# A transformer block on one core: first modulation chunk ahead of the inputs, squares summed on VectorE, one chunk ahead in a forced order, twelve ring slots

## The chip, the cores and the metric

One core of a Trainium2 chip runs the kernel. The metric is the device time of one execution in microseconds (us); lower is better. The kernel before takes 1745.03 us (median of 3 runs, 1744.43 to 1747.97).

## The reference, cut to what matters

The reference is one block of a diffusion transformer (256 tokens of x, 256 of a context, width 2048): a recurrent branch, windowed attention, a gated merge and a convolutional feed-forward, all in fp32. Only its beginning concerns this change:

```
mod = silu(cond) @ w_ada + b_ada              # six vectors of 2048, for x and for the context
def rms_norm(x, gain):   x * rsqrt(mean(x * x) + EPS) * gain
def modulate(x, gain, shift, scale):   rms_norm(x, gain) * (1 + scale) + shift
pc = modulate(ctx, norm1_g, mod_c[0], mod_c[1]) @ w_in
px = modulate(x,   norm1_g, mod_x[0], mod_x[1]) @ w_in
```

## The kernel before

Activations lie transposed: width on the 128 partitions (16 tiles, `kt`), 512 tokens (x, then context) in the free dimension. A fp32 product is taken as three products of fp32r parts: each operand is split into a high part (a cast on ScalarE) and a low part (a subtraction on VectorE); `mm3` (line 71) issues high by high, high by low, low by high. A tile framework plans the order of each engine's queue by priority, which is the order of the program text; `tc.high_priority(offset=n)` moves what stands in it n places ahead, and `tc.issue_after(ins)` queues what stands in it behind `ins` on its engine. Each engine then works through its queue in order, and SyncE's queue of transfers too.

*The modulation.* Shift and scale (4096 columns of `w_ada`) are made in eight chunks. Chunk j gives the columns of the two width tiles 2j and 2j+1, takes eight transfers of 512 KB (`ada_load`, line 170) and 32 TensorE instructions in four column groups (`ada_mm`, line 173). `mod_chunk` (line 178) copies the four rows of partial sums to SBUF, turns them into columns by products with `sel`, which also adds the four groups, and forms `acol` and `bcol` (scale with gain, and shift). Then it multiplies each x tile by the row `rs` of reciprocal norms, applies `acol` and `bcol` on ScalarE (two halves: x and context) and splits the result into `xhi` and `xlo`.

*The norm.* `x_part` (line 199) loads four x tiles by one transfer of 1 MB; ScalarE squares each tile, and a TensorE product with a matrix of ones adds it over partitions and tiles into `ssq`; `rsqrt` (line 139) makes `rs` by Ln and Exp.

*Order at the start.* Eight ring slots (two tiles of four) hold one chunk. Chunk 0's transfers are mixed with the inputs'; chunk 1 follows and is modulated (lines 206 to 220) before the j loop.

*The first products.* The loop at line 267 runs j = 0 to 7 over pairs of width tiles. `unit_v` (24 products into four PSUM banks that stay open over all j) and `unit_f` (18 products into three banks) use tiles 2j and 2j+1. Their weights come through `st.load` (line 105): a transfer, a cast and a subtraction. In between stand the two halves of chunk j+2's products and, at the end of the round, its `mod_chunk`: the modulation runs two chunks ahead. The order of the weight file `wst` (line 922) is the order of the loads.

After the loop TensorE goes on with 16-tile sums (`tform`, line 345) for the rest of the block; the other four modulation vectors are summed on VectorE meanwhile from the transfers `araw` (line 294).

Of the kernel before, what the change touches and what calls it, by code (L numbers as in the profile page):

```python
# [27 lines left out]
RUSH = 120  # L28
# [23 lines left out]
def block_kernel(ctx, tc, xct, prm, cst, ada2, wst, out):  # L52
    nc = tc.nc
    V, S, PE = nc.vector, nc.scalar, nc.tensor

    cons = ctx.enter_context(tc.tile_pool(name="cons", bufs=1))
    big = ctx.enter_context(tc.tile_pool(name="big", bufs=1))
    strm = ctx.enter_context(tc.tile_pool(name="strm", bufs=3))
    scr = ctx.enter_context(tc.tile_pool(name="scr", bufs=3))
    tiny = ctx.enter_context(tc.tile_pool(name="tiny", bufs=8))  # L60
    mm = ctx.enter_context(tc.tile_pool(name="mm", bufs=5, space=bass.MemoryType.PSUM))
    ms = ctx.enter_context(tc.tile_pool(name="ms", bufs=3, space=bass.MemoryType.PSUM))

    def bank(pool=None):
        pool = pool or mm
        return pool.tile([P, 512], F32, name="bank" + ("m" if pool is mm else "s"))

    def mmul(o, l, r, start, stop):
        PE.matmul(o, l, r, start=start, stop=stop, skip_group_check=True)  # L69

    def mm3(o, lh, ll, rh, rl, start, stop):
        mmul(o, lh, rh, start, False)
        mmul(o, lh, rl, False, False)
        mmul(o, ll, rh, False, stop)

    def smalltile(w, name="tn"):
        return tiny.tile([P, 32], F32, name=name)[:, 0:w]
# [79 lines left out]
    slots = [r[:, i, :] for r in ring for i in range(4)]  # L157


    csr = big.tile([P, KT, 32], F32, name="csr", tag="acc")  # L160
# [3 lines left out]
    sel = smalltile(2, "sel")  # L164
    V.tensor_tensor(sel, ident[:, 0:2], ident[:, 32:34], op=ALU.add)
    V.tensor_tensor(sel, sel, ident[:, 64:66], op=ALU.add)
    V.tensor_tensor(sel, sel, ident[:, 96:98], op=ALU.add)
    rs = scr.tile([P, 512], F32, name="rs", bufs=1)

    def ada_load(i):  # L170
        st.load_raw(slots[i])

    def ada_mm(aps, half):
        for kt in range(8 * half, 8 * half + 8):
            g = 32 * (kt % 4)
            mmul(aps[g:g + 32, :], csr[:, kt, :], slots[kt // 2][:, kt % 2 * 512:kt % 2 * 512 + 512], kt < 4, kt >= KT - 4)

    def mod_chunk(j, aps):
        rows = scr.tile([P, 512], F32, name="t")
        S.copy(rows, aps)  # L180
        for q in range(4):
            mmul(aps[:, 2 * q:2 * q + 2], rows[:, q * P:q * P + P], sel, q == 0, True)
        a4 = aps[:, 0:8].rearrange("p (q c) -> p q c", c=2)
        js = slice(2 * j, 2 * j + 2)
        V.tensor_tensor(bcol[:, js, :], a4[:, 0:2, :], bsh[:, js, None].broadcast_to([P, 2, 2]), op=ALU.add)
        V.tensor_tensor(acol[:, js, :], a4[:, 2:4, :], bsc[:, js, None].broadcast_to([P, 2, 2]), op=ALU.add)
        V.tensor_tensor(acol[:, js, :], acol[:, js, :], par("n1g")[:, js, None].broadcast_to([P, 2, 2]), op=ALU.mult)
        for kt in range(2 * j, 2 * j + 2):
            hn = scr.tile([P, 512], F32, name="t")
            V.tensor_tensor(hn, xraw[:, kt, :], rs, op=ALU.mult)  # L190
            for cnd in range(2):
                sl = slice(T * cnd, T * cnd + T)
                S.activation(hn[:, sl], hn[:, sl], AF.Identity, bias=bcol[:, kt, cnd:cnd + 1],
                             scale=acol[:, kt, cnd:cnd + 1])
            split(xhi[:, kt, :], xlo[:, kt, :], hn)

    ssq = bank()

    def x_part(i):
        nc.sync.dma_start(xraw[:, 4 * i:4 * i + 4, :], xct[:, 4 * i:4 * i + 4, :])  # L200
        for kt in range(4 * i, 4 * i + 4):
            sq = scr.tile([P, 512], F32, name="t")
            S.activation(sq, xraw[:, kt, :], AF.Square)
            mmul(ssq, ones, sq, kt == 0, kt == KT - 1)

    for i in range(8):
        ada_load(i)
        if i % 2:
            x_part(i // 2)
    for j in range(2):  # L210
        if j:
            for i in range(8):
                ada_load(i)
        aps = bank(ms)
        for half in range(2):
            ada_mm(aps, half)
        with tc.high_priority(offset=0 if j else RUSH):
            if not j:
                rsqrt(rs, ssq, 1.0 / D)
            mod_chunk(j, aps)  # L220
    base[0] = tc.tile_snap_priority()
    early_v = [bank() for _ in range(4)]

# [19 lines left out]
    def unit_v(j):  # L243
        st.load()
        return [st.next(4) for _ in range(2)]

    def unit_v_mm(j, wv, tts):
        for tt in tts:
            ts = slice(tt * P, tt * P + P)
            for k2 in range(2):  # L250
                kt = 2 * j + k2
                mm3(early_v[tt], xhi[:, kt, ts], xlo[:, kt, ts], *wv[k2], kt == 0, kt == KT - 1)
# [12 lines left out]


    for j in range(8):
        more = j < 6
        aps = bank(ms) if more else None
        wv = unit_v(j)  # L270
        if more:
            for i in range(4):
                ada_load(i)
        unit_v_mm(j, wv, range(4))
        if more:
            ada_mm(aps, 0)
        w = unit_f(j)
        if more:
            for i in range(4, 8):
                ada_load(i)  # L280
        unit_f_mm(j, w)
        if more:
            ada_mm(aps, 1)
            mod_chunk(j + 2, aps)
# [241 lines left out]
    kT = big.tile([P, 2, 512], F32, name="kT", tag="kT")  # L526
    va = big.tile([P, 4, 256], F32, name="va", tag="va")
# [50 lines left out]
    for h in range(H):  # L578
# [147 lines left out]
    ssa = scr.tile([P, 512], F32, name="rs", bufs=1)  # L726
# [22 lines left out]
    for j in range(W0, KT):  # L749
        o = tform(yb)  # L750
# [220 lines left out]
```

## Time and profile before

| | before |
|---|---|
| median of 3 runs | 1745.03 us |
| profiled execution | 1748.49 us |
| its span, first to last instruction | 1746.6 us |
| mean granted TensorE clock (share of 2.4 GHz) | 0.996 |
| TensorE matmul busy | 1719.9 us (98%) |
| VectorE busy | 1197.0 us (69%) |
| ScalarE busy | 847.6 us (49%) |
| mean DMA rate over the span | 213 GB/s |

PE is TensorE's matmul side, PEld its weight loads, DVE VectorE, ACT ScalarE, SP SyncE. All helpers record line 69 for a matmul, so groups of products are told apart by their tiles: `ringv,csr` and `ringq,csr` are the modulation, `t,cst` the norm, `sel,t` the turning of its rows, `whi,hl` and `wlo,hl` unit_v, `hl,whi` and `hl,wlo` unit_f and later sums. fp32 operands that are not fp32r take two instructions for one product.

### The profile page before, as it was taken

To read this page: it belongs to the slowest core of one execution; us is meant where nothing else is said; L and a number is where in the kernel's file an instruction comes from. 1 tells how busy PE (TensorE), PEld (TensorE's weight loads), DVE (VectorE), ACT (ScalarE), POOL (GpSimd) and SP (SyncE) were. 2 spreads that over 40 slices of the span, in tenths; PEclk is the share of its full clock that TensorE was granted. 3 is DMA by queue.
4 is the path that set the end of the run, shared out by engine and by line. 5 is a ranking of instruction groups with operands and counts; after the bars stand their busy time and mean duration, and the time that the engine had idled before them with its cause. 6 is when DMAs were issued, how large, how long until landed. Compare 5 with 4: busy or idle time off the path is not lost.

```text
span 1746.6 us, 24907 instructions
## 1 busy us (share of the span) xinstructions
PE 1719.9 (98%) x9562; PEld 1451.9 (83%) x9562; DVE 1197.0 (69%) x1807; ACT 847.6 (49%) x1292; POOL 68.4 (4%) x132
## 2 busy tenths in 40 slices
PE   7999999999999999999999999999999999999999
PEld 2567888888888888888888898888888888888887
DVE  1335967464669878697878797788766656666665
ACT  4335554252545755454455475555555334554332
POOL 0000100000000001010100000000000000000000
PEclk9999999999999999999999999999999999999999
DMA  9795744433436558686876567677755555555554
GB/s 374 297 364 184 265 143 157 161 117 117 136 104 214 202 189 289 233 309 237 304 249 231 190 215 256 228 239 262 233 183 186 188 185 188 183 192 182 190 196 145
DMA packets 103432, 371.85 MB, mean 213 GB/s; under 512 B 11280, under 2 KB 13712, under 8 KB 102800
## 3 DMA queue, kind: packets, MB, share of 16 engines
q1 hardware_dynamic: 84880, 303.14, 49.2%
q0 software_dynamic: 18432, 67.12, 11.8%
q8 instruction: 75, 1.23, 0.3%
q14 instruction: 45, 0.37, 0.1%
HBM read 368.11 MB, written 2.10 MB: 212 GB/s over the span
## 4 chain that ended last, share of the span: by engine, by line
PE 93%; DMA 4%; DVE 1%; issue 1%; ACT 0%; SPq 0%; DVEq 0%; POOLq 0%
PE bankm L69 84%; PE banks L69 6%; DMA araw<-in_ada_dram 3%; DVE wlo L111 1%; PE banks L493 0%; DMA raw<-in_wst_dram 0%; DVE acc L309 0%; DMA xraw<-in_xct_dram 0%; PE banks L666 0%; PE banks L317 0%; PE banks L485 0%; PE banks L475 0%; PE banks L522 0%; ACT whi L110 0%; PE banks L636 0%
## 5 line engine op out<-in xcount | busy, mean ns | idle before, releaser
L69 PE MATMUL bankm<-hl,whi 128*128 128x512 f32 (+1 forms) x3392 | 1163.3, 394 | 0.0
L69 PE MATMUL bankm<-hl,wlo 128*128 128x256 f32 (+2 forms) x3104 | 899.7, 290 | 4.1 <-DVE wlo L111 4.1
L111 DVE TENSOR_TENSOR wlo<-raw,whi 128x1024 fp32r<-128x1024 f32 x498 | 606.7, 1219 | 337.2 <-ACT whi L110 335.1
L110 ACT CAST whi<-raw 128x1024 fp32r<-128x1024 f32 x498 | 520.2, 1045 | 634.8 <-PE bankm L69 492.5
L69 PEld LDWEIGHTS bankm<-hl,whi 128*128 128x128 f32 x3392 | 633.0, 188 | 144.1
L69 PEld LDWEIGHTS bankm<-hl,wlo 128*128 128x128 f32 x3104 | 587.6, 189 | 16.4 <-DVE wlo L111 5.7
L309 DVE SCALAR_TENSOR_TENSOR acc<-araw,csil,acc 128x1024 f32<-128x1024 f32 x120 | 153.7, 1281 | 29.4 <-DMA araw<-in_ada_dram 28.6
L69 PE MATMUL bankm<-whi,hl 128*128 128x512 f32 x512 | 167.3, 400 | 6.3 <-ACT whi L110 6.3
L69 PEld LDWEIGHTS bankm<-whi,hl 128*128 128x128 f32 x512 | 96.7, 190 | 31.3 <-ACT whi L110 7.2
L304 POOL DMA_DIRECT2D araw<-in_ada_dram x128 | 68.2, 533 | 1172.5 <-DVE acc L309 671.7
L69 PE MATMUL bankm<-wlo,hl 128*128 128x512 f32 x256 | 101.2, 395 | 0.0
L69 PE MATMUL bankm<-yb,whi 128*128 128x512 f32 x256 | 91.0, 400 | 0.0
L69 PE MATMUL bankm<-g,whi 128*128 128x512 f32 x256 | 90.5, 399 | 0.0
L69 PE MATMUL bankm<-yb,wlo 128*128 128x256 f32 x256 | 72.2, 282 | 0.0
L69 PE MATMUL bankm<-g,wlo 128*128 128x256 f32 x256 | 71.9, 281 | 0.0
L813 DVE SCALAR_TENSOR_TENSOR xm<-bankm,modv,xm 128x256 f32<-128x256 f32 x96 | 46.4, 484 | 31.2 <-PE bankm L69 29.4
L69 PEld LDWEIGHTS bankm<-g,whi 128*128 128x128 f32 x256 | 48.1, 188 | 12.0
L69 PEld LDWEIGHTS bankm<-yb,whi 128*128 128x128 f32 x256 | 48.1, 188 | 11.8
L69 PEld LDWEIGHTS bankm<-wlo,hl 128*128 128x128 f32 x256 | 48.6, 190 | 10.6 <-DVE wlo L111 1.2
L69 PEld LDWEIGHTS bankm<-yb,wlo 128*128 128x128 f32 x256 | 48.4, 189 | 0.3
L69 PEld LDWEIGHTS bankm<-g,wlo 128*128 128x128 f32 x256 | 48.4, 189 | 0.0
L793 ACT ACTIVATE fs<-fs,prm 128x256 f32<-128x256 f32 x44 | 26.5, 601 | 43.7 <-DVE fs L368 43.5
(200 smaller groups left out, 1187.4 us busy)
## 6 DMA issues: line engine op xcount, KB each, us to landing
raw<-in_wst_dram SPq DMA_DIRECT2D x490, 512.0 KB, 3.4
araw<-in_ada_dram POOLq DMA_DIRECT2D x128, 512.0 KB, 4.7
ringv<-in_wst_dram SPq DMA_DIRECT2D x32, 512.0 KB, 5.9
ringq<-in_wst_dram SPq DMA_DIRECT2D x32, 512.0 KB, 6.3
xraw<-in_xct_dram SPq DMA_DIRECT2D x4, 1024.0 KB, 12.8
raw<-in_wst_dram SPq DMA_DIRECT2D x8, 384.0 KB, 7.3
xm<-in_xct_dram SPq DMA_DIRECT2D x2, 1024.0 KB, 9.1
out_dram<-xm SPq DMA_DIRECT2D x3, 512.0 KB, 3.6
```

The source lines that it names most:

```text
L69: PE.matmul(o, l, r, start=start, stop=stop, skip_group_check=True)
L110: S.copy(hi, raw)
L111: self.last = V.tensor_tensor(lo, raw, hi.bitcast(F32), op=ALU.subtract)
L304: nc.gpsimd.dma_start(raw, ada2[idx])
L309: V.scalar_tensor_tensor(acc, raw, csil[:, kt, 0:1], acc, op0=ALU.mult, op1=ALU.add)
L793: S.activation(t, s, AF.Identity, bias=cb[:, f:f + 1], scale=cw[:, f, 1:2])
L813: V.scalar_tensor_tensor(xm[:, j, :], o[:, T * i:T * i + T], gate2[:, j:j + 1], xm[:, j, :], op0=ALU.mult, op1=ALU.add)
```

## The change

The first chunk's eight transfers now come first, then the inputs (eight transfers of two tiles), then the first products' weights. The squares are added on VectorE into `ssa`, which shares the tile of `csr`, and one ones-product at the end sums over partitions. Four more ring slots are made of the two `araw` buffers and the tiles `kT` and `va`, so the ring holds three half chunks. `scale_x` multiplies a chunk's x tiles by `rs` in place, ahead of the modulation; `mod_chunk` turns the rows by four transposes and adds the groups by a VectorE reduction that reads two of 32 columns of each group; ScalarE writes `xhi` directly, and VectorE computes the same affine map in place for the subtraction. In round j of the loop the order on TensorE is forced: unit_v of j, all of chunk j+1's products, then unit_f of j; `mod_chunk(j + 1)` stands between them, 24 places ahead.

```diff
     def mod_chunk(j, aps):
         rows = scr.tile([P, 512], F32, name="t")
         S.copy(rows, aps)
         for q in range(4):
-            mmul(aps[:, 2 * q:2 * q + 2], rows[:, q * P:q * P + P], sel, q == 0, True)
+            PE.transpose(aps[:, q * P:q * P + P], rows[:, q * P:q * P + P], ident)
+        m8 = smalltile(8).rearrange("p (q c) -> p q c", c=2)
+        V.tensor_reduce(m8, aps.rearrange("p (q g c) -> p q c g", q=4, g=4)[:, :, 0:2, :], axis=AX.X, op=ALU.add)
...
         for kt in range(2 * j, 2 * j + 2):
-            hn = scr.tile([P, 512], F32, name="t")
-            V.tensor_tensor(hn, xraw[:, kt, :], rs, op=ALU.mult)
             for cnd in range(2):
-                S.activation(hn[:, sl], hn[:, sl], AF.Identity, bias=bcol[:, kt, cnd:cnd + 1],
-                             scale=acol[:, kt, cnd:cnd + 1])
-            split(xhi[:, kt, :], xlo[:, kt, :], hn)
+                xs = xraw[:, kt, T * cnd:T * cnd + T]
+                a, b = acol[:, kt, cnd:cnd + 1], bcol[:, kt, cnd:cnd + 1]
+                S.activation(xhi[:, kt, T * cnd:T * cnd + T], xs, AF.Identity, bias=b, scale=a)
+                V.tensor_scalar(xs, xs, a, b, op0=ALU.mult, op1=ALU.add)
+            V.tensor_tensor(xlo[:, kt, :], xraw[:, kt, :], xhi[:, kt, :].bitcast(F32), op=ALU.subtract)
...
             S.activation(sq, xraw[:, kt, :], AF.Square)
-            mmul(ssq, ones, sq, kt == 0, kt == KT - 1)
+            if kt:
+                V.tensor_tensor(ssa, ssa, sq, op=ALU.add)
+    def scale_x(j):
+        for kt in range(2 * j, 2 * j + 2):
+            V.tensor_tensor(xraw[:, kt, :], xraw[:, kt, :], rs, op=ALU.mult)
+    aps = bank(ms)
+    for half in range(2):
+        ada_load(0, half)
+        ada_mm(aps, 0, half)
     for i in range(8):
-        ada_load(i)
-        if i % 2:
-            x_part(i // 2)
...
+        x_part(i)
+    with tc.high_priority(offset=RUSH):
+        ssq = bank()
+        mmul(ssq, ones, ssa, True, True)
+        rsqrt(rs, ssq, 1.0 / D)
+        scale_x(0)
+        mod_chunk(0, aps)
...
     for j in range(8):
...
+        wv, w = unit_v(j), unit_f(j)
+        more = j < 7
+        unit_v_last = unit_v_mm(j, wv, range(4))
+        if not more:
+            unit_f_mm(j, w)
+            break
+        aps = bank(ms)
+        for half in range(2):
+            ada_load(j + 1, half)
+        scale_x(j + 1)
+        with tc.issue_after(unit_v_last.ins):
+            ada_mm(aps, j + 1, 0)
+            last = ada_mm(aps, j + 1, 1)
+        with tc.high_priority(offset=24):
+            mod_chunk(j + 1, aps)
+        with tc.issue_after(last.ins):
+            unit_f_mm(j, w)
```

## Rows read from the trace of the kernel before

**Rows 1.** The page's chain that ended last, by engine.
```profile
PE 93%; DMA 4%; DVE 1%; issue 1%; ACT 0%; SPq 0%; DVEq 0%; POOLq 0%
```

**Rows 2.** Windows: bounds and length; busy us (instructions); granted clock; DMA share; GB/s.
```profile
0.00:20.00 20.00, 11.31 (x29) 3.76 (x30) 2.04 (x16) 6.98 (x14) 0.20 (x4) 1.00 0.90 348
16.00:31.00 15.00, 15.00 (x50) 5.01 (x49) 0.00 (x0) 7.33 (x12) 0.00 (x0) 1.00 1.02 421
41.40:47.70 6.30, 0.01 (x1) 0.02 (x1) 1.42 (x3) 3.48 (x6) 0.00 (x0) 0.82 1.02 410
47.70:52.10 4.40, 4.36 (x9) 2.97 (x10) 2.15 (x2) 1.65 (x2) 0.00 (x0) 0.50 1.02 417
62.88:77.55 14.67, 14.67 (x87) 9.46 (x83) 5.17 (x10) 5.70 (x9) 0.00 (x0) 1.00 0.88 314
...
136.40:157.60 21.20, 20.52 (x93) 16.82 (x94) 10.08 (x18) 14.02 (x22) 0.66 (x1) 1.00 0.40 131
```

**Rows 3.** Chain of waits in order of time: start us, us, what.
```profile
38.56 8.01 DMA raw<-in_wst_dram
...
46.59 1.05 ACT whi L110
...
47.69 1.22 PE bankm L69 x2
...
267.10 0.55 PE banks L317 x5
```

**Rows 4.** Timeline of TensorE: start us, us, operation [idle before].
```profile
27.37 3.70 PE L69 MATMUL bankm<-t,cst 128*128 128x512 f32 x8
...
55.72 1.07 PE L69 MATMUL banks<-ringv,csr 128*32 128x512 f32 x8
...
62.88 0.50 PE L69 MATMUL bankm<-whi,hl 128*128 128x512 f32 x1
...
63.93 0.95 PE L69 MATMUL banks<-sel,t 128*128 128x2 f32 x8
...
69.49 1.92 PE L69 MATMUL banks<-ringv,csr 128*32 128x512 f32 x16
71.35 0.74 PE L69 MATMUL banks<-hl,whi 128*128 128x512 f32 x2
...
75.69 1.92 PE L69 MATMUL banks<-ringq,csr 128*32 128x512 f32 x16
...
137.08 1.05 PE L69 MATMUL banks<-sel,t 128*128 128x2 f32 x8 [0.71 <-ACT t L180]
...
157.52 0.39 PE L69 MATMUL bankm<-hl,whi 128*128 128x512 f32 x1
```

**Rows 5.** DMA issues until 40 us: tile, queue, count, KB each, us to landing.
```profile
ringv<-in_wst_dram SPq DMA_DIRECT2D x11, 512.0 KB, 9.3
xraw<-in_xct_dram SPq DMA_DIRECT2D x4, 1024.0 KB, 12.8
```

**Rows 6.** Groups by line and form until 160 us: count, busy us, mean ns.
```profile
L131 DVE TENSOR_TENSOR hl<-t,hl 128x512 fp32r<-128x512 f32 x16 | 11.1, 692 | 15.9 <-ACT hl L130 15.8
L190 DVE TENSOR_TENSOR t<-xraw,rs 128x512 f32<-128x512 f32 x16 | 10.4, 684 | 0.0
...
L203 ACT ACTIVATE t<-xraw 128x512 f32<-128x512 f32 x16 | 9.6, 625 | 14.8 <-DMA xraw<-in_xct_dram 8.0 <-PE bankm L69 6.8
```

**Rows 7.** One line each: count, duration min/median/max in ns, first and last start.
```profile
L318 DVE TENSOR_REDUCE modv<-banks x16: 674/682/692, 267.6 to 1290.2; 128x4 f32<-128x512 f32 x16
...
L761 ACT ACTIVATE hl<-xa,modv x16: 494/498/520, 1006.3 to 1020.9; 128x256 fp32r<-128x256 f32 x16
```

**Rows 8.** Timeline of ScalarE and VectorE in one round: start us, us, operation.
```profile
63.04 0.59 ACT L180 COPY t<-banks 128x512 f32<-128x512 f32 x1 [1.09 <-PE banks L69]
64.99 0.16 DVE L185 TENSOR_TENSOR bcol<-banks,prm 128x4 f32<-128x4 f32 x1 [0.57 <-PE banks L69]
...
68.74 0.69 DVE L131 TENSOR_TENSOR hl<-t,hl 128x512 fp32r<-128x512 f32 x1 [0.47 <-ACT hl L130]
```

More of the change, by code (lines that the diff above doesn't have):

```diff
@@ L68, in mmul @@
     def mmul(o, l, r, start, stop):
-        PE.matmul(o, l, r, start=start, stop=stop, skip_group_check=True)
+        return PE.matmul(o, l, r, start=start, stop=stop, skip_group_check=True)
     def mm3(o, lh, ll, rh, rl, start, stop):
@@ L73, in mm3 @@
         mmul(o, lh, rl, False, False)
-        mmul(o, ll, rh, False, stop)
+        return mmul(o, ll, rh, False, stop)
     def smalltile(w, name="tn"):
@@ L156, in block_kernel, with ada_load, ada_mm @@
     ring = [big.tile([P, 4, 1024], F32, name="ringv", tag="v"), big.tile([P, 4, 1024], F32, name="ringq", tag="qo")]
-    slots = [r[:, i, :] for r in ring for i in range(4)]
-    csr = big.tile([P, KT, 32], F32, name="csr", tag="acc")
+    spare = [strm.tile([P, 1024], F32, name="araw", bufs=2) for _ in range(2)]
+    spare += [big.tile([P, 1024], F32, name="ring" + t, tag=t) for t in ("kT", "va")]
+    slots = [[r[:, i, :] for i in range(4)] for r in ring] + [spare]
+    start = big.tile([P, 1024], F32, name="csr", tag="acc")
+    csr, ssa = start[:, 0:512].rearrange("p (k c) -> p k c", c=32), start[:, 512:]
     V.tensor_scalar(csr, one_c[:, None, :].broadcast_to([P, KT, 32]), 0.0, None, op0=ALU.mult)
     V.tensor_copy(csr[:, :, 0:2], csil)
[L164 to L167, printed above, removed]
     rs = scr.tile([P, 512], F32, name="rs", bufs=1)
-    def ada_load(i):
-        st.load_raw(slots[i])
-    def ada_mm(aps, half):
+    def ada_load(j, half):
+        for slot in slots[(2 * j + half) % 3]:
+            st.load_raw(slot)
+    def ada_mm(aps, j, half):
         for kt in range(8 * half, 8 * half + 8):
-            g = 32 * (kt % 4)
-            mmul(aps[g:g + 32, :], csr[:, kt, :], slots[kt // 2][:, kt % 2 * 512:kt % 2 * 512 + 512], kt < 4, kt >= KT - 4)
+            g, c = 32 * (kt % 4), kt % 2 * 512
+            last_mm = mmul(aps[g:g + 32, :], csr[:, kt, :], slots[(2 * j + half) % 3][kt % 8 // 2][:, c:c + 512], kt < 4, kt >= KT - 4)
+        return last_mm
     def mod_chunk(j, aps):
@@ L186, in mod_chunk @@
-        V.tensor_tensor(acol[:, js, :], a4[:, 2:4, :], bsc[:, js, None].broadcast_to([P, 2, 2]), op=ALU.add)
+        V.tensor_tensor(acol[:, js, :], m8[:, 2:4, :], bsc[:, js, None].broadcast_to([P, 2, 2]), op=ALU.add)
         V.tensor_tensor(acol[:, js, :], acol[:, js, :], par("n1g")[:, js, None].broadcast_to([P, 2, 2]), op=ALU.mult)
+        V.tensor_tensor(bcol[:, js, :], m8[:, 0:2, :], bsh[:, js, None].broadcast_to([P, 2, 2]), op=ALU.add)
         for kt in range(2 * j, 2 * j + 2):
-            hn = scr.tile([P, 512], F32, name="t")
-            V.tensor_tensor(hn, xraw[:, kt, :], rs, op=ALU.mult)
@@ L199, in x_part @@
+                V.tensor_scalar(xs, xs, a, b, op0=ALU.mult, op1=ALU.add)
+            V.tensor_tensor(xlo[:, kt, :], xraw[:, kt, :], xhi[:, kt, :].bitcast(F32), op=ALU.subtract)
     def x_part(i):
-        nc.sync.dma_start(xraw[:, 4 * i:4 * i + 4, :], xct[:, 4 * i:4 * i + 4, :])
-        for kt in range(4 * i, 4 * i + 4):
-            sq = scr.tile([P, 512], F32, name="t")
+        nc.sync.dma_start(xraw[:, 2 * i:2 * i + 2, :], xct[:, 2 * i:2 * i + 2, :])
+        for kt in range(2 * i, 2 * i + 2):
+            sq = scr.tile([P, 512], F32, name="t") if kt else ssa
@@ L203, in x_part @@
             S.activation(sq, xraw[:, kt, :], AF.Square)
-            mmul(ssq, ones, sq, kt == 0, kt == KT - 1)
-    for i in range(8):
-        ada_load(i)
-        if i % 2:
-            x_part(i // 2)
[L210 to L220, printed above, removed]
+            if kt:
+                V.tensor_tensor(ssa, ssa, sq, op=ALU.add)
@@ L251, in unit_v_mm @@
                 kt = 2 * j + k2
-                mm3(early_v[tt], xhi[:, kt, ts], xlo[:, kt, ts], *wv[k2], kt == 0, kt == KT - 1)
+                last_mm = mm3(early_v[tt], xhi[:, kt, ts], xlo[:, kt, ts], *wv[k2], kt == 0, kt == KT - 1)
+        return last_mm
     def unit_f(j):
@@ L267, in block_kernel @@
     for j in range(8):
[L268 to L284, printed above, removed]
+        wv, w = unit_v(j), unit_f(j)
[15 more added lines that the diff above has]
+            unit_f_mm(j, w)
     vn = big.tile([P, 4, 1024], F32, name="vn", tag="v")
@@ L921 @@
     first = np.stack([fft[0], fbt[0], fft[1]], 0).transpose(1, 0, 2, 3)
-    parts = [ada1[0], ada1[1]]
+    parts = [ada1[0]]
     for j in range(8):
-        more = ada1[j + 2] if j < 6 else ada1[0:0, 0]
-        parts += [vh[0, j][None], more[0:4]]
         t6 = first[2 * j:2 * j + 2].reshape(6, P, P)
-        parts += [_halves(np, np.concatenate([t6, np.zeros((2, P, P), np.float32)], 0)), more[4:8]]
+        parts += [vh[0, j][None], _halves(np, np.concatenate([t6, np.zeros((2, P, P), np.float32)], 0))]
+        if j < 7:
+            parts.append(ada1[j + 1])
     parts.append(_halves(np, qt))
```

4 lines of the change are left out of this document (removed).

## The prediction, made before the change was run

> **What bounds the kernel now.** I read the page's chain that ended last first: TensorE carries 93% of it [rows 1]. So a change to the first 160 us pays only if it lets TensorE begin its long unbroken work earlier, or takes TensorE work out of it. Next come the windows by stage [rows 2]. Until 31 us the stage is bound by transfers (16 to 31 us: DMA share 1.02, 421 GB/s). From 41.4 to 47.7 us TensorE does nothing while DMA runs at 410 GB/s. From about 62 us to the end of the first products each round of the j loop takes 14.67 us (this row; four in a row do) with TensorE busy for all of it, at full clock, and DMA, in the one of 62.88, at 314 GB/s, under the 421 it had before: there TensorE sets the pace. The chain in order of time names what ends the front [rows 3]: a weight transfer issued at 38.56 us takes 8.01 us to land, because it stands in SyncE's queue behind two whole chunks of modulation weights and the inputs; then its cast, and the first product at 47.69 us. The first products end at 157.52 us, where the first product of the next stage starts [rows 4].
>
> **The change part by part.**
>
> *Order of the transfers.* Ahead of the first product's weights there now lie chunk 0 (8 x 512 KB), the inputs (4 x 1024 KB), chunk 1 and a part of chunk 2. After the change there lie only chunk 0 and the inputs. The pieces are 8 x 512 and 4 x 1024 KB [rows 5]; the two parameter loads ahead of them (lines 82 and 83: 635 and 256 columns of 128 floats) make 317.5 and 128. Together 8637.5 KB, or 8.84 MB. The first 20 us bring 20 x 348 = 6.96 MB [rows 2]; the remaining 1.88 MB at 421 GB/s take 4.5 us, so the inputs are in at 24.5 us, say 25 with the last landing. The weights for j = 0 (512 and 384 KB) follow within 2.2 us, chunk 1 (4.19 MB) within another 10, at 37 us. The loads of chunk 1 no longer wait for ring slots: its first half has the four new slots, its second half the slots that the first half of chunk 0 left long before. The inputs come in eight pieces of 512 KB where they came in four of 1024; the ring's pieces are 512 KB too and the queue is full at 421 GB/s with them, so I put that at nothing (bounds: nothing, and 0.5 us, one more issue time, since all the others lie beside transfers).
>
> *Norm of the inputs.* 16 x 2 ones-products (0.43 us each, 3.70 us for 8 [rows 4]) leave TensorE, 14 us in all; they lie wholly in the front, beside transfers, so their absence alone gives nothing. In their place are 15 additions on VectorE (0.69 us each by the nearest row, the 128x512 subtraction of line 131, [rows 6]; they start some 0.6 us apart) against an arrival of two tiles each 1.25 us (524 KB at 421 GB/s): they just keep up. After the last landing at 25.0 us: two squares 0.63 + 0.52, the last addition 0.69, to 26.9. One ones-product in two passes: TensorE has been idle by then, so I take 0.86 us each, twice the warm 0.43: to 28.7. Ln and Exp of 128x512, at the square's 0.63 or a little more, with their starts 1.35, to 30.05. The first scaling by rs 0.68 to 30.8, then 0.5 for the first activation. Chunk 0's copy, transposes and reduction need only the modulation weights and are done before. First product: 31.3 us; I take 31.5, with 30.5 and 34 as ends (34 if a cast or the copy stands ahead of a square in ScalarE's queue, or all four activations and both subtractions, 4 x 0.5 + 0.69, must come first). Now it is 47.7: 16.2 us earlier.
>
> *The clock at the start.* Without the ones-products TensorE has no work from about 16 us, when chunk 0 is consumed, to 27. That is no new loss for the first products: they start after 6.3 us of idleness today as well, and the row for 47.7 to 52.1 us shows a granted clock of 0.50, the 1.2 GHz level [rows 2]. So I carry over today's length of the first unit_v, 47.69 to 55.72, 8.0 us.
>
> *One round.* TensorE's work in it: unit_v, 24 products. Today they take 62.88 to 69.49, 6.61 us, with eight products by sel in between [rows 4]; unit_f has 18 in 4.34, 0.24 each, so 24 take 5.6 to 5.8; I take 5.6 and 1.0 for the sel part. The modulation products are unchanged, 2 x 1.86, less one change of form, 3.6. unit_f 4.34. Four transposes by 0.11 (five in 0.55 us [rows 3]) 0.44. Sum 14.0 against 14.67. All eight rounds from the first product: 8.0 + 3.6 + 4.8 for j = 0, 6 x 14.0, and 9.9 for j = 7, which has no chunk: 110.3 us. Today it is 157.5 - 47.7 = 109.8, with two chunks done before the first product and six after it, where it will be one and seven. So TensorE's work from the first product on stays equal and the end moves with the start.
>
> *The wait that is added.* Today chunk j+2 is modulated during round j, a full round ahead. After the change chunk j+1 is modulated in round j, and unit_v of round j+1 needs it at once. What covers it is unit_f of round j and the transposes: 4.8 us. The chain, from the end of the modulation products, by today's rows [rows 8]: copy begins 0.16 later and takes 0.59; four transposes, to 1.35; the reduction reads 32 elements per partition out of PSUM (nearest rows: 0.16 us for 4 elements, line 185 [rows 8], and 0.68 for 512, line 318 [rows 7]; I take 0.25) and begins 0.3 after the products, as line 185 does: 1.9; the three small operations to 2.3; four activations 0.5 apart write xhi, to 4.4 (line 761 has this form, 0.498 us [rows 7]); VectorE computes the same in place (0.34 each, half of line 190's 0.68 for double the length [rows 6]) and subtracts (0.69): first tile of xlo at 4.4, second at 5.7. unit_v can start at 4.8 with the first tile and wants the second's xlo with its sixth product, 1.2 us on, at 6.0. So the chain just fits, with 0.3 us to spare. What can stand ahead in the in-order queues is a cast of weights on ScalarE (1.05 [rows 3]), their subtraction on VectorE (bounded below by 0.69 for half the length, above by twice that) or the two scalings (0.68 each); all three are free to run earlier in the round, when their data are there. I put the stall at 0.5 us a round, 3.5 in all. Lower end 0. Upper end: today's chain in full, 63.04 to 69.43, 6.4 us, less the 4.8 of cover, rounded up to 1.8 with the start of the copy, 12.6 in all.
>
> *Transfers in a round.* 8 x 512 + 512 + 384 KB = 5.11 MB, 12.2 us at 421 GB/s, under the 14.0 of TensorE. With twelve slots half a chunk waits for the half three before it. Chunk 7 is in at 25 + (44.6 - 8.84 MB) / 421 GB/s = 110 us and wanted at about 125, so the queue is throttled by slots and not late.
>
> *Behind it.* What follows starts from TensorE's progress: a weight's cast waits for a buffer that products release, and the later modulation's steps are queued behind a weight's subtraction (`issue_after(st.last)`). So I take all of it as moved whole; 1 us either way for a changed order is a guess.
>
> **Sum.** Start -16.2, work from there +0.5, stalls +3.5: -12.2 us. The profiled execution took 1748.5 us (span 1746.6 and 1.9 around it): 1736.3. It lay 3.5 us above the median of the three runs, so by the median 1745.0 - 12.2 = 1732.8, rounded to 1733.
>
> **Rivals.** *The modulation chain is not covered (slower).* If the four transposes are placed behind unit_f in TensorE's queue, the rest of the chain, some 4.5 us (5.7 less the copy and transposes, and the wait for xlo that the first products cover), stands open each round: 7 x 4.5 = 31.5 less 12.2 and the 3.5 already counted, +16: 1761. The point from which it decides is 2.3 us of stall a round (16.2 - 0.5 over 7). For it: one chunk ahead, and only 0.3 us to spare. Against: today's order puts the sel products three products behind the modulation products, just as the copy ends [rows 4, 8], and unit_f stands behind them by priority.
>
> *Gaps cost the clock.* A gap each round might drop TensorE to half speed each time. Round 7 shows a gap of 0.71 us before the sel products [rows 4], and the clock of 136.4 to 157.6 us stayed at 1.00 [rows 2]; 6.3 us did drop it. By those rows, a fall would cost half of the 4.4 us at 0.50, 2.2, and 7 x 2.2 = 15.4 would make 1748. The Trainium skill (TensorE: Matmul & The Clock Gate, section HAM oscillation) describes this rule, that bursts of matmuls parted by waits start throttled again and again; by it the change would be worth nothing. Here the expected gaps are at or under the one that left the clock up, so I give it little.
>
> *The gain is halved.* A late start (34), 1.5 us of stall a round, or a stream that falls back towards the 314 GB/s of a round today: at 340 chunk 7 would land at 25 + 35.8 / 0.34 = 130, 5 us after it is wanted. Each leaves 3 to 8 us: 1737 to 1742.
>
> *It gives more.* No stall and the start at 30.5: 16.7 us, and at most another in the stage behind: 1728.
>
> **How the numbers follow.** Forecast with its own 8.5 to 16 us of gain, 1729 to 1736.5: 0.66. Halved gain: 0.19, of which 0.05 stay within 0.2% (3.5 us, about what a measurement here can tell from no change). More: 0.05. Chain open, or clock lost: 0.10, of which 0.02 at no change. Faster 0.66 + 0.14 + 0.05 = 0.85, same 0.07, slower 0.08. The range takes the ends of start and stall, 1728 to 1742, and leaves out the open chain and the lost clock: about 0.85, of which I call 0.8.
>
> **What would show it.** Right: the first product of unit_v at 31 to 32 us; DMA at about 420 GB/s from 10 to 37 us; rounds of 14.0 to 14.5 us with the transposes three or four products into unit_f; the first product of the next stage at 142 to 147 us; the rest as before. Wrong: a wait of TensorE for hl longer than 1 us each round; a clock of 0.50 in the rounds; a wait for the ring; or a first product after 36 us, with squares or casts standing in ScalarE's queue behind a transfer.

## The result and the profile after

The changed kernel takes 1731.24 us (median of 4 runs, 1730.87 to 1735.77); the kernel before, on the same chip, 1746.50 (4 runs, 1744.43 to 1750.88). The ratio is 0.9915, with a 95% interval of 0.9889 to 0.9942: faster by about 15 us, where 12.2 were forecast, and 1.8 us under the forecast time. The profiled execution took 1731.31 us (span 1729.5, clock 0.994) against 1748.49 before.

The page after: busy times, and the chain that ended last by engine.

```profile
PE 1696.3 (98%) x9500; PEld 1440.9 (83%) x9500; DVE 1216.4 (70%) x1859; ACT 837.4 (48%) x1276; POOL 68.7 (4%) x132
...
PE 72%; issue 16%; DMA 7%; DVE 4%; ACT 1%; POOL 0%; SPq 0%; DVEq 0%; POOLq 0%; ACTq 0%
```

TensorE is busy for 1696.3 us, 23.6 less than before; some 12 of it are the ones-products (14 us, less the 2.07 of the one that is left). The chain's TensorE share fell from 93% [rows 1] mostly into "issue", time for which the profile shows no releaser, so the page alone doesn't say what was gained. The stages do. The windows after (bounds and length, busy us of each engine, granted clock, DMA share, GB/s):

```profile
16.00:30.00 14.00, 1.22 (x5) 0.18 (x1) 10.38 (x15) 11.16 (x18) 0.00 (x0) 0.60 1.02 419
...
34.87:42.56 7.69, 7.69 (x24) 5.91 (x24) 7.69 (x18) 3.20 (x5) 0.00 (x0) 0.71 1.03 418
...
51.79:65.51 13.72, 13.67 (x76) 8.62 (x76) 3.77 (x10) 2.92 (x5) 0.00 (x0) 1.00 0.88 344
78.80:92.60 13.80, 13.80 (x80) 9.15 (x79) 5.17 (x13) 4.34 (x8) 0.00 (x0) 1.00 0.99 390
...
684.00:700.00 16.00, 13.94 (x79) 11.77 (x78) 9.37 (x10) 6.94 (x9) 0.53 (x1) 1.00 0.78 270
```

Against [rows 2]: TensorE now idles for most of 16 to 30 us (busy 1.22) while transfers run at 419 GB/s; the granted clock, 0.60 on average there, is 0.50 from 18.8 us on, when the first products come. The first unit_v (34.87 to 42.56) passes from half to full clock, mean 0.71. From 51.79 us on the rounds take 13.72 to 13.94 us each, 13.8 on average, where they took 14.67. The window from 78.80 us is as long as a round, and TensorE is busy for all of it.

The chain of waits after, in order of time (start us, us, what), answers to [rows 3]:

```profile
6.70 10.21 DMA xraw<-in_xct_dram
...
18.11 0.70 DVE csr L206
...
18.91 0.70 DVE csr L206
19.70 0.70 DVE csr L206
...
29.25 0.70 DVE csr L206
30.00 2.09 PE bankm L69 x2
32.11 0.70 ACT rs L140
32.83 0.64 ACT rs L141
33.49 1.29 DVE xraw L210 x2
```

The weight transfer that ended the front is gone from it. In its place stand the fifteen additions of squares from 18.11 to 29.95 us, one after the other, then the ones-product, Ln, Exp and the first scalings.

The timeline of TensorE after (start us, us, operation, idle before and its releaser) answers to [rows 4]:

```profile
34.87 0.80 PE L69 MATMUL bankm<-whi,hl 128*128 128x512 f32 x1 [2.16 <-ACT hl L194]
...
51.79 0.73 PE L69 MATMUL bankm<-whi,hl 128*128 128x512 f32 x2 [0.34 <-DVE hl L196]
...
57.05 1.92 PE L69 MATMUL banks<-ringq,csr 128*32 128x512 f32 x16
...
60.62 0.73 PE L69 MATMUL banks<-hl,whi 128*128 128x512 f32 x2
...
61.65 0.60 PE L183 MATMUL banks<-cst,t 128*128 128x128 f32 x4
...
144.14 0.39 PE L69 MATMUL bankm<-hl,whi 128*128 128x512 f32 x1
...
687.68 0.39 PE L69 MATMUL bankm<-hl,wlo 128*128 128x256 f32 x1 [1.49 <-DVE wlo L111]
```

The first unit_v starts at 34.87 (before 47.69), the next stage at 144.14 (before 157.52). A round's 32 modulation products are one block (57.05 to 60.62), and the transposes follow four products into unit_f. Seven changes from unit_f to unit_v leave one wait, 0.34 us.

So of the 17.1 us between the two spans, 13.4 are there at the next stage. The other 3.7 appear behind it, where the order of each engine's queue is the same in both kernels. In the profile of before two windows behind 200 us have the clock at half level for most of their length:

```profile
202.30:206.00 3.70, 3.70 (x14) 3.14 (x13) 3.70 (x6) 2.05 (x4) 1.03 (x2) 0.54 0.66 229
704.00:707.70 3.70, 3.70 (x14) 3.11 (x13) 2.19 (x2) 3.17 (x5) 0.00 (x0) 0.54 0.68 252
```

Each costs 3.70 x (1 - 0.54) = 1.7 us, 3.4 together. They follow waits of TensorE, 0.86 and 2.13 us long in the timeline of before:

```profile
199.32 0.89 PE L69 MATMUL banks<-hb 128*128 128x64 f32 x4 [0.86 <-DVE hb L496]
...
703.17 0.39 PE L69 MATMUL bankm<-hl,wlo 128*128 128x256 f32 x1 [2.13 <-DVE wlo L111]
```

The execution of after has no such stretch; its waits at the same two places are 1.06 and 1.49 us. The change doesn't rule them out: e5 below, with the same order behind 145 us, has two of them again. Whether it makes them rarer stays open. The mean granted clock of before in its 57 later runs has the median 0.996, that of the profiled execution, whose front alone gives 0.998; the four runs of after have 0.994, 0.994, 0.993 and 0.992, where the front alone gives 0.994 (0.001 is 1.7 us). By the medians, 15.3 us apart, 1.9 lie behind the front.

### The profile page after: what moved, and what is told of

It is laid out like the page before. It is cut to its first block, busy times and chain, and to the rows that moved or that the text cites. A ratio compares the mean times of both kernels' runs of the same rounds, so it can differ in the third digit from the quotient of the medians.

```text
span 1729.5 us, 24839 instructions
## 1 busy us (share of the span) xinstructions
PE 1696.3 (98%) x9500; PEld 1440.9 (83%) x9500; DVE 1216.4 (70%) x1859; ACT 837.4 (48%) x1276; POOL 68.7 (4%) x132
## 3 DMA queue, kind: packets, MB, share of 16 engines
q0 software_dynamic: 18432, 67.12, 12.2%
## 4 chain that ended last, share of the span: by engine, by line
PE 72%; issue 16%; DMA 7%; DVE 4%; ACT 1%; POOL 0%; SPq 0%; DVEq 0%; POOLq 0%; ACTq 0%
PE bankm L69 67%; DMA araw<-in_ada_dram 6%; PE banks L69 4%; DVE wlo L111 1%; DVE acc L313 1%; DVE csr L206 1%; DMA xraw<-in_xct_dram 1%; DVE xraw L210 1%; POOL araw L308 0%; PE banks L497 0%; PE banks L321 0%; DMA ringv<-in_wst_dram 0%; PE banks L489 0%; PE banks L479 0%; ACT whi L110 0%
```

## The experiments

Each is an edit of the changed kernel; "next stage" is its first product (144.14 us there). Before ran with each group: its median was 1745.78 us in the first four, 1743.74 in the next and 1745.12 in the last four, so ratios are compared across groups, not times. The groups are e1 to e4, e5 to e8, e9 to e12. Starts are read from one profiled execution each: with the same front (after, e5, e7, e9, e10) the first unit_v lies between 34.87 and 35.53, so differences under 0.7 us there say nothing.

### The sum of squares: e1, e2, e6

e1: two squares of a transfer are added, and TensorE sums eight pairs.

```diff
-            sq = scr.tile([P, 512], F32, name="t") if kt else ssa
...
-                V.tensor_tensor(ssa, ssa, sq, op=ALU.add)
+        V.tensor_tensor(sq, sq, sr, op=ALU.add)
+        mmul(ssq, ones, sq, i == 0, i == 7)
```

> Theory A: the first product waits for the running sum on VectorE: fifteen additions into one tile, each waiting for the one before, start 0.79 us apart (18.11 to 29.25 us) while the inputs come every 0.62 us. Here each transfer's two squares are added to each other (eight additions that do not depend on one another) and eight ones-products on TensorE sum them up. By A the last ones-product ends about 28.5 us, where the single one ended at 32.1; unit_v starts at about 31.3 in place of 34.87, and with TensorE already busy it runs partly at the full clock; the execution takes 3.5 to 5 us less than the changed kernel's 1731, about 1727. Rival B: the landing of the inputs and the weights sets the start; then nothing moves: 34 to 35 us for the first product, 1731.

Measured: 1735.44 us, ratio 0.9947 (0.9931 to 0.9963); first unit_v at 35.48, next stage 145.04. A miss: the squares share three scratch tiles, two now held per pair, so ScalarE waited for TensorE's products and the last pair was summed at 31.61. The edit changed the buffers as well as the sum, and said nothing on the theory.

e2: all sixteen squares go to TensorE, as before the change.

```diff
-            if kt:
-                V.tensor_tensor(ssa, ssa, sq, op=ALU.add)
+            mmul(ssq, ones, sq, kt == 0, kt == KT - 1)
```

> Here every square goes to a ones-product on TensorE again (16 x 2, as in the kernel before), all else stays as changed. Theory A (the move of the squares is worth nothing by itself, the transfers' order is the gain): the products start at 17 us, half clock at first, then 0.86 us each, and end at 32 to 33.5, near the 32.1 of the changed kernel; unit_v starts at 34 to 36 but at the full clock, 2 us shorter: 1729 to 1732. Rival C: the 14 us of ones-products taken off TensorE are a main part of the gain; then the first products end 8 to 14 us later: 1739 to 1745.

Measured: 1733.06 us, ratio 0.9941 (0.9926 to 0.9957); next stage 144.71. The timeline of TensorE in e2:

```profile
17.95 14.00 PE L69 MATMUL bankm<-t,cst 128*128 128x512 f32 x32 [0.85 <-ACT t L206]
...
34.75 0.50 PE L69 MATMUL bankm<-whi,hl 128*128 128x512 f32 x1 [2.36 <-ACT hl L194]
...
50.12 0.50 PE L69 MATMUL bankm<-whi,hl 128*128 128x512 f32 x1 [0.82 <-ACT hl L194]
...
51.79 0.73 PE L69 MATMUL bankm<-whi,hl 128*128 128x512 f32 x2 [0.93 <-DVE hl L196]
```

The 14 us of products end at 31.95, as late as VectorE's sum and its one product, and the next stage starts 0.6 us later than in the changed kernel. So moving the squares was worth nothing by itself that can be told: theory A, though the total is 1 us over its range. With TensorE at full clock the first unit_v takes 6.1 us instead of 7.7, and yet the second begins in full at the same 51.79: something else holds it (e5, e12).

e6: the squares get a tile in the memory that `hl` takes later, so no buffer holds ScalarE back; pairs are added independently, TensorE sums eight; the scalings are kept in their round (e5).

```diff
+    sqs = big.tile([P, KT, 512], F32, name="sqs", tag="hl")
...
+            S.activation(sqs[:, kt, :], xraw[:, kt, :], AF.Square)
+        V.tensor_tensor(sqs[:, 2 * i, :], sqs[:, 2 * i, :], sqs[:, 2 * i + 1, :], op=ALU.add)
+        mmul(ssq, ones, sqs[:, 2 * i, :], i == 0, i == 7)
```

> The changed kernel with two parts changed: the sixteen squares get a tile of their own (in the memory that hl takes later), so ScalarE never waits for VectorE; VectorE adds two squares of one transfer (eight additions that don't depend on each other) and TensorE sums the eight pairs; and the scalings are kept in their round as in the run before. Theory A (the first product was late against the forecast because of the running sum, each addition waiting for the one before, 0.79 us a tile): last of the ones-products at 28.5 to 29, first unit_v at 31.2 to 31.8 us (3.1 to 3.7 earlier than 34.87), TensorE warm in it (6.1 to 6.6 us where it took 7.7), first product of the next stage at 138.5 to 141, total 1726 to 1728. Rival B (the start is bound by weights or by casts, not by the sum): first unit_v not before 34 us, total within 1 us of the changed kernel. Rival C (the start is earlier but the second chunk or the next weights aren't there: they land by 37 to 38 us either way): a wait of 2 to 3 us ahead of the second unit_v, total 1729 to 1731.

Measured: first unit_v at 32.45, 2.4 us earlier (expected 3.1 to 3.7); next stage 140.99; 1729.39 us, ratio 0.9914 (0.9899 to 0.9928). The timeline of ScalarE, VectorE and TensorE in e6:

```profile
19.77 7.75 ACT L203 ACTIVATE sqs<-xraw 128x512 f32<-128x512 f32 x14
...
21.68 7.97 PE L69 MATMUL bankm<-sqs,cst 128*128 128x512 f32 x14 [0.28 <-DVE sqs L204]
...
27.55 0.69 DVE L204 TENSOR_TENSOR sqs<-sqs 128x512 f32<-128x512 f32 x1 [0.55 <-ACT sqs L203]
...
32.45 0.80 PE L69 MATMUL bankm<-whi,hl 128*128 128x512 f32 x1 [2.80 <-ACT hl L191]
```

The last addition ends at 28.24 where the chained sum ended at 29.95, and the front ends 3.1 us earlier: the chained sum did hold the start. Now ScalarE's squares, without a gap from 19.77 to 27.52, set it. In the total, 1.4 us over theory A's range, these 3.1 us can't be told: the intervals of e6 and of the changed kernel lie over each other. In its profiled execution a wait of 2.6 us at 181.8 and a stretch at half clock behind it took more than that back; whether that is regular these runs don't settle.

### What stands in VectorE's queue: e3, e8, e5, e12

e3: chunk 1's transfers go ahead of the first products' weights.

```diff
+    for half in range(2):
+        ada_load(1, half)
...
-        for half in range(2):
+        for half in range(2 if j else 0):
...
```

> Chunk 1's eight transfers stand ahead of the first products' weights; all else as changed. Theory A (the transfers' order is the gain): 4.19 MB at 420 GB/s are 10 us more before the weights, which land at about 36.7 in place of 27; after the cast the first product starts at 38 to 39 us, 3 to 4 us later than 34.87: 1734 to 1736. Rival: the weights are not what is late, 1731.

Measured: 1742.51 us, ratio 0.9986 (0.9975 to 0.9996). The first unit_v is at 38.19, as expected; the total is 6.5 us over its range, and the next stage is at 155.0, 10.9 us late where 3.3 were the start's. The timeline of VectorE and TensorE in e3:

```profile
38.97 5.50 DVE L210 TENSOR_TENSOR xraw<-xraw,rs 128x512 f32<-128x512 f32 x9
44.39 2.08 DVE L111 TENSOR_TENSOR wlo<-raw,whi 128x1024 fp32r<-128x1024 f32 x2
...
45.66 0.79 PE L69 MATMUL bankm<-wlo,hl 128*128 128x512 f32 x1 [5.82 <-DVE wlo L111]
```

`scale_x` of all later rounds needs only `rs` and the inputs. It is ready at 34 us, and the planner puts it into VectorE's in-order queue at once, here ahead of the weights' subtraction: TensorE waits 5.82 us. The same block stands in the changed kernel (timeline of VectorE after):

```profile
18.11 11.84 DVE L206 TENSOR_TENSOR csr<-csr,t 128x512 f32<-128x512 f32 x15 [12.99 <-ACT t L204]
...
40.22 6.71 DVE L210 TENSOR_TENSOR xraw<-xraw,rs 128x512 f32<-128x512 f32 x11
46.85 2.08 DVE L111 TENSOR_TENSOR wlo<-raw,whi 128x1024 fp32r<-128x1024 f32 x2
48.85 0.18 DVE L185 TENSOR_REDUCE tn<-banks 128x8 f32<-128x32 f32 x1
```

Chunk 1's reduction waits there behind the block and two subtractions until 48.85. e5 keeps the scalings in their round:

```diff
-        scale_x(j + 1)
+        with tc.issue_after(st.last.ins):
+            scale_x(j + 1)
```

> The changed kernel with one order changed: the sixteen scalings xraw*rs of round j are allowed into VectorE's queue only after the weight subtraction of that round, so that in round 0 they no longer stand as one block (6.7 us for 11) ahead of chunk 1's chain. Theory A (the block cost only the one wait of 0.34 us that TensorE shows at 51.79 us): first product of unit_v stays at 34.9, second unit_v at 51.4 to 51.8, rounds stay 13.7 to 13.8 us, first product of the next stage 143.5 to 144.2 us, total 0 to 1 us under the changed kernel. Rival B (the block hides a longer delay of all weights in round 0): second unit_v 1 to 2 us earlier, total 2 us under. Rival C (the scalings, kept in their round, now stand ahead of the last conversions of each round): a new wait of 0.7 to 1.4 us in each round, total 5 to 9 us over.

Measured: 1731.27 us, ratio 0.9922 (0.9909 to 0.9935). The first wait is gone, another of 0.60 us stands at 66.30, next stage 144.97. Within the measurement that is no change, nearest to theory A. In the changed kernel the first unit_v runs partly at half clock (0.71), so TensorE comes late to the second, and the block cost it almost nothing.

e8 is e3 with e5's edit:

```diff
+    for half in range(2):
+        ada_load(1, half)
...
+        with tc.issue_after(st.last.ins):
+            scale_x(j + 1)
...
```

> The changed kernel with chunk 1's transfers ahead of the first products' weights, and the scalings kept in their round. It is the earlier run with late weights (first unit_v 38.19, first product of the next stage 155.0 against 144.1) without the block of scalings ahead of the weights' subtraction. Theory A (of those 10.9 us only 3.3 were the order of the transfers, the rest was the block of scalings that stood ahead of the weights' subtraction on VectorE): first unit_v at 38 to 38.5, no wait over 1 us for wlo behind it, first product of the next stage at 147 to 149, total 1734 to 1736. Rival B (the loss comes from the transfers themselves: the weights of the first unit_f lie still further behind): a wait of 4 us or more remains, next stage at 152 or later, total 1739 to 1742.

Measured: 1736.56 us, ratio 0.9954 (0.9937 to 0.9970); first unit_v 38.53, next stage 149.85. The wait of 5.82 us is gone and so are 5.15 of the 10.9 us. The other 5.7 are the start (3.7) and 2.0 between: the first unit_v takes 8.9 us, at a mean clock of 0.64 where the changed kernel has 0.71, and rounds about 14.2 where 13.8 are usual, which stays unexplained. The times lie between the two theories' ends, nearer to A.

e12 is e2 with e5's edit (the same two lines).

> The changed kernel with all sixteen squares summed on TensorE, as before the change, and the scalings kept in their round. It is the earlier run with ones-products, whose unit_v of round 0 ran at full clock (6.1 us where it took 7.7) and whose second unit_v yet began at the same 51.8 us, without the block of scalings on VectorE. Theory A (that block is what gave the 1.6 us back): first unit_v at 34.7 to 35.3, second unit_v at 50 to 50.6, first product of the next stage 142 to 143 us, total 1728.5 to 1730.5. Rival B (chunk 1's chain is bound by its transfers, not by VectorE): second unit_v at 51.5 or later, next stage at 144 or later, total 1731 to 1733.

Measured: first unit_v 35.14, 5.7 us long, second at 49.12 without a wait, next stage 142.36: theory A as to the front. The timeline of TensorE in e12:

```profile
49.12 0.39 PE L69 MATMUL bankm<-whi,hl 128*128 128x512 f32 x1
```

So with TensorE at full clock the block costs 2.35 us (144.71 in e2). And with the scalings kept in their round the squares on TensorE bring the next stage 1.8 us earlier than the changed kernel does; the totals don't tell the two apart. The total, 1731.81 us, ratio 0.9922 (0.9905 to 0.9939), is 1.3 us over its expectation, which the front doesn't explain.

### Slots: e4, e7

e4 leaves out the four added slots:

```diff
...
-    slots = [[r[:, i, :] for i in range(4)] for r in ring] + [spare]
+    slots = [[r[:, i, :] for i in range(4)] for r in ring]
...
```

> A ring of eight slots, so that a half chunk waits for the half two before it; all else as changed. My reckoning: a chunk's transfers can begin only when the chunk before is being consumed and take 12.2 us with the weights at 420 GB/s, plus some 2 us to land, in a round of 13.8: it just fits or misses by up to 1.5 us a round, 0 to 10 us in all, 3 as a guess (1734). Rival: the twelve slots carry the gain, since without them the stream stalls for 2 us and more each round: 1745. Other rival: they are worth nothing: 1731.

Measured: 1739.86 us, ratio 0.9974 (0.9956 to 0.9992); first unit_v 37.93, next stage 152.86. But the planner had now put the first weights behind chunk 1's transfers, so it is e3's fault again and tells nothing of slots. e7 has eight slots too and holds the order:

```diff
...
+        with tc.issue_after(st.dma.ins):
+            for half in range(2):
+                ada_load(j + 1, half)
```

> The changed kernel with eight ring slots in place of twelve and the order of SyncE's queue held as it is (weights of a round ahead of the next chunk's transfers). Theory A (the four extra slots only let transfers run ahead, TensorE sets the pace): first unit_v at 34.9, second at 51.8 to 52.5, rounds 13.8 to 14.1 us, total 0 to 3 us over the changed kernel. Rival B (the slots are what allows one chunk ahead: with eight, a half chunk waits for the half two before it, so in each round the second half lands late): a wait of TensorE for the ring of 1 to 2 us in each round, total 8 to 14 us over.

Measured: 1730.58 us, ratio 0.9926 (0.9908 to 0.9943), next stage 143.37. The window of one round in e7:

```profile
78.68:92.49 13.81, 13.81 (x80) 9.14 (x78) 5.19 (x13) 4.37 (x9) 0.00 (x0) 1.00 1.01 398
```

TensorE is busy for all of it with eight slots too. The four slots are worth nothing measurable.

### The round: e9, e10, e11

e9 makes the forecast's slower rival: the transposes stand behind unit_f.

```diff
+            f_last = unit_f_mm(j, w)
+        with tc.high_priority(offset=24), tc.issue_after(f_last.ins):
+            mod_chunk(j + 1, aps)
```

> The changed kernel with the four transposes of a chunk placed behind unit_f in TensorE's queue, so that copy, transposes, reduction and conversions of chunk j+1 are no longer covered by the 18 products of unit_f. It is the slower rival of the forecast, made on purpose. Theory A (the rival's price was right: the chain stands open each round and nothing else takes its place): a wait of TensorE of 3.5 to 4.5 us ahead of unit_v in each of 7 rounds, at full clock, rounds of 17 to 18 us, first product of the next stage at 168 to 176, total 1756 to 1763. Rival B (waits of that length also cost the clock in each round, 1.7 us of lost time for each, as after the waits of 0.9 and 2.1 us at 198 and 701 us in the kernel before): granted clock 0.50 for some 3.4 us at the start of each unit_v, total 1766 to 1775. Rival C (the chain is short when nothing stands in it): waits of 1.5 to 2.5 us, total 1741 to 1749.

Measured: 1745.27 us, ratio 0.9997 (0.9983 to 1.0011); next stage 155.37. The timeline of one round's end in e9:

```profile
66.97 0.60 PE L183 MATMUL banks<-cst,t 128*128 128x128 f32 x4
67.61 0.19 DVE L185 TENSOR_REDUCE tn<-banks 128x8 f32<-128x32 f32 x1 [2.37 <-PE banks L183]
...
68.22 2.08 ACT L194 ACTIVATE hl<-xraw,bcol,acol 128x256 fp32r<-128x256 f32 x4 [3.98 <-DVE acol L188]
...
68.88 0.50 PE L69 MATMUL bankm<-whi,hl 128*128 128x512 f32 x1 [1.31 <-ACT hl L194]
```

and a window of a round in e9:

```profile
68.88:84.26 15.38, 14.07 (x79) 9.17 (x79) 5.59 (x13) 4.46 (x8) 0.00 (x0) 1.00 0.88 340
```

The open chain costs 1.31 us (1.38 in the first of seven rounds), not the 3.5 to 4.5 of A and under C's 1.5: unit_v needs only the first of the four activations, and its products cover the others and the subtractions. With this wait, and the transposes no longer between products, the round is 1.6 us longer, seven times 11. By the totals (0.9997 against 0.9915) all of the gain, some 14 us, is gone; the 3 that the front doesn't have lie behind it and stay unexplained. The total is in C's range. The clock stays at 1.00 in the rounds, so B is wrong here.

e10 takes the forced order on TensorE away:

```diff
-        with tc.issue_after(unit_v_last.ins):
-            ada_mm(aps, j + 1, 0)
-            last = ada_mm(aps, j + 1, 1)
+        ada_mm(aps, j + 1, 0)
+        last = ada_mm(aps, j + 1, 1)
...
-        with tc.issue_after(last.ins):
-            unit_f_mm(j, w)
+        unit_f_mm(j, w)
```

> The changed kernel without the two forced orders on TensorE (modulation products behind unit_v, unit_f behind the modulation products); the planner sets the order by priority and readiness. Theory A (the forced order is what covers the chain of chunk j+1 with unit_f): unit_f is taken ahead of the modulation products in most rounds, since its weights are there first; the chain then stands open, 3 us or more of wait in each round, total 1748 to 1760. Rival B (the transfers and priorities give the same order anyway): the same sequence of phases, total within 1 us of the changed kernel (1730 to 1732.5).

Measured: 1766.61 us, ratio 1.0113 (1.0094 to 1.0133), the one clearly slower; next stage 175.18. Both theories miss. The timeline of TensorE in one round (87.00 to 106.51, 19.5 us) of e10:

```profile
87.00 0.74 PE L69 MATMUL bankm<-whi,hl 128*128 128x512 f32 x2 [1.14 <-ACT hl L194]
...
90.27 1.06 PE L69 MATMUL banks<-araw,csr 128*32 128x512 f32 x6
91.26 0.50 PE L69 MATMUL banks<-hl,whi 128*128 128x512 f32 x1
...
97.84 1.05 PE L69 MATMUL banks<-ringv,csr 128*32 128x512 f32 x4
98.83 0.72 PE L69 MATMUL banks<-hl,whi 128*128 128x512 f32 x2
...
100.64 1.05 PE L69 MATMUL banks<-ringv,csr 128*32 128x512 f32 x4
```

The wait is only 1.14 us. The round's 32 modulation products stand in six blocks, and these take 1.04 + 1.06 + 1.91 + 1.05 + 1.05 + 1.05 = 7.2 us where one block takes 3.6 (57.05 to 60.69 after); four alone cost 1.05, while sixteen in a row cost 1.92. So 3.5 of the 5.7 us more are the blocks, 1.1 the wait, and the rest lies in the products between. The forced order is worth 35 us, 31 of them in the front, for the most part by keeping forms apart. The Trainium skill, TensorEngine Tiling (Array Packing), section Key Properties, says that a change of tiling mode drains TensorE. These rows fit that: each block of 32-column products added costs some 0.7 us (3.5 over five).

e11 brings the products by `sel` back for the transposes and the reduction:

```diff
...
-            PE.transpose(aps[:, q * P:q * P + P], rows[:, q * P:q * P + P], ident)
-        m8 = smalltile(8).rearrange("p (q c) -> p q c", c=2)
-        V.tensor_reduce(m8, aps.rearrange("p (q g c) -> p q c g", q=4, g=4)[:, :, 0:2, :], axis=AX.X, op=ALU.add)
+            mmul(aps[:, 2 * q:2 * q + 2], rows[:, q * P:q * P + P], sel, q == 0, True)
+        m8 = aps[:, 0:8].rearrange("p (q c) -> p q c", c=2)
```

> The changed kernel with the old form of a chunk's last step: eight products by sel (the sum over four groups and the turn in one) in place of four transposes and a reduction on VectorE. Theory A (TensorE sets the pace and pays for eight products of some 0.12 us each where it now pays four transposes of 0.11 to 0.15): 0.4 us more a round, 3 us in all, rounds 14.1 to 14.2, total 1733 to 1735. Rival B (the chain, shorter by the reduction, starts the conversions earlier, which gives nothing since no wait is left, while the products lie in TensorE's idle slots): total within 1 us of the changed kernel.

Measured: 1741.41 us, ratio 0.9976 (0.9966 to 0.9986); first unit_v 36.47, next stage 150.38. Eight sel products take 0.95 us where four transposes take 0.60, stand at half clock ahead of the ones-product at the start (1.6 us), and leave a wait of 0.22 to 0.25 us for the subtraction in later rounds. These are most of the 6.2 us in the front, more than either theory has; the other 4 us of the total lie behind it and stay unexplained.

## Why the prediction was right, step by step

The mechanism held: the inputs' norm, not a weight transfer, now lets TensorE begin, its work from there is nearly as long as before (109.3 against 109.8 us), and what follows moves as a whole. Over the changed kernel, before and the twelve experiments the next stage starts between 141.0 and 175.2 us, while median time less that start stays between 1586.3 and 1591.4. That the transfers' order alone makes the earlier start is read from the two chains; e3 tests it with one of the two chunks put back ahead of the weights (3.3 us), and no run undoes it whole. Nor does one take back the affine map that VectorE now computes in place. The terms:

| step | predicted | measured |
|---|---|---|
| inputs landed | 24.5 to 25 us | 25.7 (last issue 15.7, 10.0 to landing) |
| last addition ends | 26.9 | 29.95 |
| ones-product ends | 28.7 | 32.07 |
| first unit_v starts | 31.5 (30.5 to 34) | 34.87 |
| first unit_v, length | 8.0 | 7.7 |
| a round | 14.0 | 13.72 to 13.94, mean 13.8 |
| stalls in all | 3.5 | 0.34 |
| next stage | 142 to 147 | 144.14 |
| behind it | moved whole | 3.7 less in the profile, 1.9 by the medians |

*Start: mis-sized by 3.4 us, outside its ends.* The step that was mis-sized is "they start some 0.6 us apart ... they just keep up". That is the distance of operations that don't wait for each other: the eleven independent scalings of the same size take 6.71 us, 0.60 apart. Here each addition takes the sum that the last one wrote, and they start 0.79 to 0.80 us apart (18.11, 18.91, 19.70 in the chain after), though each lasts 0.70. Fifteen additions cost 0.2 x 14 = 2.8 us more than counted, and the sum becomes the pace: ScalarE waits for it. e6, with eight additions that don't wait for each other, ends 1.7 us earlier. Of the 3.4 us 0.7 are the later landing, 2.35 the sum, and the rest the ones-product, 2.07 where 1.72 was taken. Nor were chunk 0's copy, transposes and reduction "done before": the copy stood behind the squares at 28.44, three transposes behind the ones-product at 31.87. It cost nothing, since their last result, at 33.36, was 0.1 us ahead of `rs`.

*Length from there: shorter by 4.5 us.* 109.27 against 110.3 + 3.5. Six rounds take 82.8 us instead of 84.0 and the last 9.5 instead of 9.9, the first 0.2 more without its stall: 1.4 together. The other 3.2 are stalls that weren't there. That "the chain just fits" was right as to what came, transposes four products into unit_f (the forecast read three from the rows of before, where there are four too), but not in its terms. The timeline of ScalarE and VectorE after, in a round whose modulation products end at 88.6:

```profile
89.20 1.05 ACT L110 CAST whi<-raw 128x1024 fp32r<-128x1024 f32 x1
...
90.79 1.22 DVE L111 TENSOR_TENSOR wlo<-raw,whi 128x1024 fp32r<-128x1024 f32 x1
...
93.80 0.68 DVE L196 TENSOR_TENSOR hl<-xraw,hl 128x512 fp32r<-128x512 f32 x1
```

Casts and subtractions of weights do stand in the chain, and the first `xlo` is there at 94.48, 5.9 us behind the modulation products where 4.4 were taken. TensorE doesn't wait all the same: unit_v starts on `xhi` at 93.23 and has begun six products by 94.48. In e11 it waits for `xlo` only behind eight.

The two errors, 3.4 us more and 4.5 less, nearly cancel: -12.8 - 0.55 = -13.4 at the next stage, where -12.2 was forecast. That the sum came so near is luck; the path was not.

*Costs put at nothing.* The smaller transfers and the slots were so (419 GB/s; e7). The scalings "are free to run earlier" was taken as harmless; they ran too early, in one block. With the first unit_v partly at half clock that cost 0.34 us; with it at full clock 2.35 (e2 against e12), and in e3 5.15 (against e8).

*Rivals.* The open chain, made in e9, gives no change, not 1761: its price of 4.5 us a round was the mis-sized term, at 1.6 measured, under the 2.3 from which it would decide. The lost clock doesn't come at the seven waits of 1.31 to 1.38 us in e9, but it is real elsewhere in this kernel: half-level stretches behind 0.86 and 2.13 us, at 1.7 us each (the forecast's estimate was 2.2). What the Trainium skill (TensorE: Matmul & The Clock Gate, section HAM oscillation) describes, bursts parted by waits that start throttled again and again, these rounds don't show; in the stage behind, single waits were followed by a fall. The larger danger, products of two forms mixed on TensorE (e10), wasn't among the rivals.

## What to carry to other kernels

Price a running sum by rows of operations that depend on each other: independent ones of the same size start closer together (here 0.60 us against 0.80). Before moving work that is ready early, look at which in-order queue it will enter and what will stand behind it; and when a test changes buffers or slots, see whether the planner moved a queue too. On TensorE keep products of different tile shapes in long blocks: here that order was worth twice the whole change.

## What the runs showed of the hardware

Falls of the clock to its lower level (0.50, 1.2 GHz) do not follow from the length of the wait alone. Two windows of e5 behind waits of 0.46 (at 184.77 us) and 2.29 us (at 686.74):

```profile
187.30:190.70 3.40, 3.40 (x14) 3.11 (x14) 3.40 (x5) 1.47 (x4) 0.53 (x1) 0.51 0.61 193
...
689.00:692.50 3.50, 3.47 (x11) 2.99 (x12) 1.44 (x2) 3.15 (x4) 0.00 (x0) 0.52 0.85 290
```

A wait of 0.46 us was followed by a fall, while 1.06 and 1.49 us in the changed kernel (684 to 700 us: clock 1.00) and 1.31 to 1.38 us seven times in e9 were not. What else decides, and why the times behind the front differ by up to 5 us, stays open.
